# A row maximum compared with the sink as a per-partition scalar, and the attention mask cast once, early, and kept

## The chip, the cores and the metric

The kernel runs on one core of one Trainium2 chip. The metric is the device time of one execution in microseconds (us). Before the change it was 3202.52 us, the median of three runs (3199.64 to 3203.96). Engines are named as in the profile: PE is TensorE, DVE is VectorE, ACT is ScalarE, POOL is GpSimd, SP is SyncE, which issues all the DMAs here.

## What is computed

One step of a two-layer backbone over 1024 latent tokens and 128 context tokens. Layer 0 mixes tokens by differential attention, layer 1 by windowed attention with grouped heads and a sink; a SwiGLU FFN follows each. The change is in layer 1's attention of the latent tokens, where 16 query heads share 4 key/value heads and every block of 128 queries sees 256 cached keys and up to three blocks of its own neighbourhood:

```python
def sink_softmax(s, sink):
    sk = sink.astype(jnp.float32).reshape(SWA_KV_HEADS, SWA_GROUP)[None, :, :, None, None]
    m = jnp.maximum(jnp.max(s, axis=-1, keepdims=True), sk)
    e = jnp.exp(s - m)
    return e / (jnp.sum(e, axis=-1, keepdims=True) + jnp.exp(sk - m))
...
valid = ((k_pos[None, :] >= 0) & (k_pos[None, :] < L)
         & (jnp.abs(q_pos[:, None] - k_pos[None, :]) <= WINDOW))
s_lat = jnp.where(valid, s_lat, NEG_INF)
p = sink_softmax(jnp.concatenate([s_ctx, s_lat], axis=-1), sink).astype(v.dtype)
```

## The kernel before, in words

The program runs in stages: layer 0's modulation and projection (`Start`, `Qkv`), its attention (`diff_attention`), output projection and FFN, then layer 1's projection, its attention (`swa_attention`), output projection and FFN. PE, DVE, ACT and POOL follow the order in which the code is written in most stages (`manual_schedule`); SP is left to the scheduler in all but the first piece.

`swa_attention` cuts the latent work into 32 units: 4 key/value heads times 8 query blocks, with 4 heads in a unit. The string `ROUND` is written out by hand and says which step of which unit is issued next; the last digit of a token is how many units it lies back. For each head of a unit:

- `step_S` (L1015, L1018, L1021) has PE write the scores into one of two PSUM tiles `S`: two matmuls over the cached keys, two over the neighbours, and a bf16 matmul of `mask` by `ident_b` that adds minus 1e30 outside the window. Every `S` ends with that matmul.
- `step_R` (L1026, L1027) has DVE reduce `S` to the negated row maximum `nm`, one number per partition, and then take the smaller of `nm` and the negated sink.
- `step_E` (L1030) has ACT compute the exponential of `S` with `nm` as bias, and the sums. Then `S` is free for the next head.

Then PE transposes the exponentials (L1050), ACT and DVE or POOL split them into a high and a low part (L1059, L1062, L1073; key blocks 0 and 2 go to POOL by L110 and L1073), PE multiplies by V (L1082, L1083), and after a second transposition (L1093, L1098) POOL scales by the reciprocal of the denominator `den` (L1042, L1043, L1102). In every second unit POOL also splits a piece of the output weights (token `W00`, `wo_piece`, L110 and L1114).

At the start of `swa_attention` SP loads the mask (L987), ACT casts it to bf16 (L988) and casts the identity too (L990). `negsink`, the negated sinks of 16 heads on every partition, is made in `small_params`, which is called in the middle of layer 0's projection (slot 20). `junk` is a tile for unwanted elementwise results: `sumsq` (L127) has ACT write squares into it.

Of the kernel before, what the change touches and what calls it, by code (L numbers as in the profile page):

```python
# [9 lines left out]
F32 = mybir.dt.float32  # L10
F32R = mybir.dt.float32r
BF16 = mybir.dt.bfloat16
AF = mybir.ActivationFunctionType
ALU = mybir.AluOpType
# [4 lines left out]
P = 128  # L19
# [25 lines left out]
def hybrid_step(ctx: ExitStack, tc: tile.TileContext, x_prompt, x_sample, cache_diff_k, cache_diff_v,  # L45
# [5 lines left out]
    act, dve, pool, pe = nc.scalar, nc.vector, nc.gpsimd, nc.tensor  # L51
    dma = nc.sync.dma_start
# [15 lines left out]
    const = ctx.enter_context(tc.tile_pool(name="const", bufs=1))  # L68
    ident = const.tile([P, P], F32, name="ident")
# [14 lines left out]
    subg = const.tile([P, 1], F32, name="subg")  # L84
    neglam = const.tile([P, 1], F32, name="neglam")
    negsink = const.tile([P, SH], F32, name="negsink")

    def sbuf(name, side=None):
        return tc.tile_pool(name=name, bufs=1, side=side, reuse_waits="tile")

    def psum(name):
        return tc.tile_pool(name=name, bufs=1, space=PSUM, reuse_waits="tile")
# [348 lines left out]

    def small_params(sb):

        dma(out=subg, in_=diff_subln_g.rearrange("o p -> p o"))
        act.mul(out=subg, in_=subg, mul=1.0 - LAM_INIT)
        lp = sb.tile([P, 4, HD], F32, name="lp")
        dma(out=lp, in_=diff_lambda.rearrange("o f d -> o (f d)").broadcast_to([P, 4 * HD]).rearrange(
            "p (f d) -> p f d", d=HD))
        lpp = sb.tile([P, 2, HD], F32, name="lpp")
        dve.tensor_tensor(out=lpp, in0=lp[:, 0:4:2, :], in1=lp[:, 1:4:2, :], op=ALU.mult)  # L450
        le = sb.tile([P, 2], F32, name="le")
        dve.tensor_reduce(out=le, in_=lpp, axis=AX.X, op=ALU.add)
        act.activation(out=le, in_=le, func=AF.Exp)
        dve.tensor_tensor(out=neglam, in0=le[:, 1:2], in1=le[:, 0:1], op=ALU.subtract)
        dve.tensor_scalar(out=neglam, in0=neglam, scalar1=-LAM_INIT, scalar2=None, op0=ALU.add)
        dma(out=negsink, in_=swa_sink.broadcast_to([P, SH]))
        act.mul(out=negsink, in_=negsink, mul=-1.0)
# [523 lines left out]

    def swa_attention(op, wo_pool, pre, kv0, q0):
        with sbuf("sa") as sb, psum("sap") as ps:

            mask = sb.tile([P, 2, P], BF16, name="mask")
            mraw = sb.tile([P, 2, P], F32, name="mraw")
            dma(out=mraw, in_=swa_mask)  # L987
            act.copy(out=mask, in_=mraw)  # L988
            ident_b = sb.tile([P, P], BF16, name="ident_b")
            act.copy(out=ident_b, in_=ident)  # L990

            class Unit:


# [29 lines left out]
                def step_R(self, h):  # L1024
                    hs, nm = self.g * SG + h, self.nm[:, h:h + 1]
                    dve.tensor_reduce(out=nm, in_=self.S[h][:, self.c0:self.c1], axis=AX.X, op=ALU.max, negate=True)  # L1026
                    dve.tensor_tensor(out=nm, in0=nm, in1=negsink[:, hs:hs + 1], op=ALU.min)  # L1027

                def step_E(self, h):
                    act.activation(out=self.e[:, h, 0:self.nk], in_=self.S[h][:, self.c0:self.c1], func=AF.Exp,  # L1030
# [700 lines left out]
    junk = const.tile([P, D], F32, name="junk")  # L1731
# [126 lines left out]
    with psum("gp0") as ps, sbuf("hT0", "left") as hp, sbuf("wq0", "left") as wq:  # L1858
# [3 lines left out]
        with ExitStack() as early, sbuf("qkv") as sb:  # L1862
# [7 lines left out]
            hooks = {i: ([], [lambda i=i: first.norm(i + 3), lambda i=i: first.load(i + 4)],  # L1870
                         lambda i=i: first.rest(i + 1)) for i in range(NTB)}
            hooks[20] = ([], [lambda: small_params(st)])
            pre0 = []

# [70 lines left out]
    mid.close()  # L1945
    la = Layer(1, pre1)
    la.wo_tiles = swa_attention(la.op, la.wp, *pre1)
    la.begin(ctx)
    before1.close()
# [51 lines left out]
```

## Time and profile before

| | |
|---|---|
| median of three runs | 3202.52 us |
| the profiled execution, its own time | 3199.07 us |
| its span | 3197.3 us |
| PE, DVE, ACT, POOL busy | 3001.8, 2048.6, 1421.9, 1361.9 us |
| granted TensorE clock, mean of the span | 0.981 of full |
| layer 1's latent attention | about 1972 to 2246 us of the span |

The profile is of one execution, so sums are made against 3199.07 us; the median of the runs lies 3.45 us above it. A busy PE is one whose matmuls are in flight, not one at its peak. [...]

### The profile page before, as it was taken

The page shows a single profiled execution, that of the slowest core. Times are in us where ns is not written, and L with a number is a line of the kernel's source. Part 1 is how long each engine was busy: PE and PEld are TensorE (multiplying, and loading weights), DVE is VectorE, ACT ScalarE, POOL GpSimd, SP SyncE. Part 2 cuts the span into 40 slices and gives each one's busy share as a digit, 9 for nine tenths or more (in the row PEclk, how much of TensorE's full clock was granted, in tenths as well). Part 3 has the DMA queues.
Part 4 walks back from the last instruction along what each step waited for, and adds up shares of the span by engine and source line. Part 5 has one row for each costly group of instructions (what it writes and reads, how often), then busy time and mean ns, then how long its engine had stood idle before and what let it go on. Part 6 is the DMA issues. An engine that isn't in the chain of part 4 may idle for free.

```text
span 3197.3 us, 47914 instructions
## 1 busy us (share of the span) xinstructions
PE 3001.8 (94%) x17998; PEld 2636.8 (82%) x17998; DVE 2048.6 (64%) x2789; ACT 1421.9 (44%) x2764; POOL 1361.9 (43%) x1186
## 2 busy tenths in 40 slices
PE   8999988998896999999999899999987999999999
PEld 5888777777776999999878787777767999998887
DVE  6786388888566777753786643999567633334544
ACT  6332267777554333333444323777433333333442
POOL 2553289999343444442021343666333433340101
PEclk9999999999998999999999999999988999999999
DMA  6675633332422434335765354433432322226564
GB/s 214 200 228 179 201 112 114 116 118 94 130 100 80 129 109 129 109 97 177 252 216 195 130 173 125 116 115 99 142 107 81 108 64 83 66 80 211 185 199 149
DMA packets 373808, 442.23 MB, mean 138 GB/s; under 512 B 26804, under 2 KB 295644, under 8 KB 373576
## 3 DMA queue, kind: packets, MB, share of 16 engines
q1 hardware_dynamic: 373576, 439.16, 43.6%
q8 instruction: 142, 2.33, 0.3%
q14 instruction: 90, 0.74, 0.1%
HBM read 335.71 MB, written 103.37 MB: 137 GB/s over the span
## 4 chain that ended last, share of the span: by engine, by line
PE 67%; POOL 14%; DVE 9%; ACT 4%; issue 3%; DMA 2%; SPq 1%; DVEq 0%; ACTq 0%; POOLq 0%
POOL aT L784 7%; PE guX L1518 6%; PE guX L1519 6%; PE guX L1520 6%; PE dacc L1635 5%; PE dacc L1637 5%; PE dacc L1636 5%; POOL aT L110 4%; PE qacc L556 4%; PE qacc L558 4%; PE qacc L557 4%; PE guY L1518 3%; PE guY L1520 3%; PE guY L1519 3%; PE guZ L1518 1%
## 5 line engine op out<-in xcount | busy, mean ns | idle before, releaser
L1551 POOL TENSOR_TENSOR sg<-sg,U 128x256 f32<-128x256 f32 x88 | 74.9, 851 | 563.4 <-ACT sg L1550 553.1
L1635 PE MATMUL dacc<-fh,ahl 128*128 128x512 f32 x792 | 312.0, 394 | 2.3 <-DVE U L1554 2.3
L1636 PE MATMUL dacc<-fl,ahl 128*128 128x512 f32 x792 | 310.7, 392 | 0.0
L1637 PE MATMUL dacc<-fh,ahl 128*128 128x512 f32 x792 | 310.7, 392 | 0.0
L556 PE MATMUL qacc<-whi,hh 128*128 128x512 f32 x648 | 259.7, 401 | 1.3 <-ACT hh L431 1.3
L558 PE MATMUL qacc<-whi,hl 128*128 128x512 f32 x648 | 254.9, 393 | 0.0
L557 PE MATMUL qacc<-wlo,hh 128*128 128x512 f32 x648 | 254.2, 392 | 0.6 <-DVE wlo L106 0.6
L154 POOL TENSOR_TENSOR xt<-yacc,xt 128x1024 f32<-128x1024 f32 (+1 forms) x19 | 49.7, 2621 | 459.9 <-DVE yacc L153 242.0
L784 POOL TENSOR_TENSOR aT<-a,aT 128x512 fp32r<-128x512 f32 x186 | 237.3, 1276 | 15.5
L1620 DVE TENSOR_TENSOR fl<-fraw,fh 128x1024 fp32r<-128x1024 f32 x132 | 165.4, 1253 | 121.3 <-ACT fh L1619 120.7
L744 DVE TENSOR_REDUCE nm<-S 128x1 f32<-128x1280 f32 x128 | 190.2, 1486 | 51.1 <-PE S L737 51.1
L1619 ACT CAST fh<-fraw 128x1024 fp32r<-128x1024 f32 x132 | 138.4, 1048 | 170.8 <-DMA fraw<-in_w_down_dram 156.7
L737 PE MATMUL S<-K,q 128*128 128x512 f32 (+1 forms) x768 | 184.5, 377 | 12.9 <-ACT e L749 8.9
L266 DVE SCALAR_TENSOR_TENSOR macc<-wmod,sc,macc 128x512 f32<-128x512 f32 x196 | 186.1, 992 | 0.0
L1635 PEld LDWEIGHTS dacc<-fh,ahl 128*128 128x128 f32 x792 | 149.2, 188 | 36.4 <-DVE U L1554 3.1
L1637 PEld LDWEIGHTS dacc<-fh,ahl 128*128 128x128 f32 x792 | 149.0, 188 | 33.7
L1636 PEld LDWEIGHTS dacc<-fl,ahl 128*128 128x128 f32 x792 | 149.1, 188 | 32.9
L749 ACT ACTIVATE e<-S,nm 128x1280 f32<-128x1280 f32 x128 | 171.4, 1339 | 7.2 <-DVE nm L744 7.1
L737 PEld LDWEIGHTS S<-K,q 128*128 128x128 f32 x768 | 137.5, 193 | 43.8 <-ACT e L749 19.0
L578 ACT CAST xT<-tpx 128x512 fp32r<-128x512 f32 x127 | 68.5, 592 | 236.5 <-issue 125.3
L110 POOL TENSOR_SCALAR aT<-a 128x512 fp32r<-128x512 f32 x192 | 154.0, 802 | 22.7 <-ACT a L773 22.7
L1490 DVE TENSOR_TENSOR fl<-fsum,fh 128x1024 fp32r<-128x1024 f32 x84 | 102.3, 1218 | 81.3 <-ACT fh L1488 81.3
(369 smaller groups left out, 9726.7 us busy)
## 6 DMA issues: line engine op xcount, KB each, us to landing
fraw<-in_w_down_dram SPq DMA_DIRECT2D x132, 512.0 KB
wmod<-in_w_mod_dram SPq DMA_DIRECT2D x112, 256.0 KB
araw<-a_d SPq DMA_DIRECT2D x132, 192.0 KB
fraw<-in_w_gate_dram SPq DMA_DIRECT2D x44, 512.0 KB
fraw<-in_w_up_dram SPq DMA_DIRECT2D x42, 512.0 KB
qT_d<-xT SPq DMA_DIRECT2D x36, 512.0 KB
q<-qT_d SPq DMA_DIRECT2D x64, 256.0 KB
wraw<-in_w_qkv_diff_dram SPq DMA_DIRECT2D x24, 512.0 KB
```

The lines of the kernel that those rows point to most:

```text
L110: pool.tensor_scalar(out=out, in0=in_, scalar1=1.0, scalar2=0.0, op0=ALU.mult, op1=ALU.add)
L556: pe.matmul(acc, lhsT=xh, rhs=hi[:, a, :], start=(kb == 0), stop=False)
L557: pe.matmul(acc, lhsT=xh, rhs=lo[:, a, :], start=False, stop=False)
L558: pe.matmul(acc, lhsT=xl, rhs=hi[:, a, :], start=False, stop=(kb == KB - 1))
L737: pe.matmul(S[:, j:j + n], lhsT=self.q[:, f, m, i * P:(i + 1) * P], rhs=kv[self.h][0][:, m, j:j + n], start=(f == 0), stop=(f == 1))
L784: (dve if self.last else pool).tensor_tensor(out=lo, in0=x, in1=hi.bitcast(F32), op=ALU.subtract)
L1518: pe.matmul(o, lhsT=hi[:, kb, :], rhs=xh[:, kb, :], start=(first and kb == 0), stop=False, **more)
L1519: pe.matmul(o, lhsT=hi[:, kb, :], rhs=xl[:, kb, :], start=False, stop=False, **more)
L1520: pe.matmul(o, lhsT=lo[:, kb, :], rhs=xh[:, kb, :], start=False, stop=(kb == 3), **more)
L1635: pe.matmul(acc, lhsT=ah, rhs=hi[:, cs], start=(d == 0), stop=False)
L1636: pe.matmul(acc, lhsT=ah, rhs=lo[:, cs], start=False, stop=False)
L1637: pe.matmul(acc, lhsT=al, rhs=hi[:, cs], start=False, stop=(d == NDF - 1))
```

## The change

The mask and the bf16 identity become tiles that live as long as the program. They are made in `small_params`, with `junk` as the landing place of the raw mask. The comparison of the maximum with the sink becomes a tensor_scalar: `negsink`'s column is the scalar operand, one value per partition, where it was a second tensor of one element per partition.

```diff
@@ hybrid_step, constants
+    mask = const.tile([P, 2, P], BF16, name="mask")
+    ident_b = const.tile([P, P], BF16, name="ident_b")
@@ small_params
+        mraw = junk[:, 0:2 * P].rearrange("p (a k) -> p a k", k=P)
+        dma(out=mraw, in_=swa_mask)
+        act.copy(out=mask, in_=mraw)
+        act.copy(out=ident_b, in_=ident)
         dma(out=subg, in_=diff_subln_g.rearrange("o p -> p o"))
@@ swa_attention
-            mask = sb.tile([P, 2, P], BF16, name="mask")
-            mraw = sb.tile([P, 2, P], F32, name="mraw")
-            dma(out=mraw, in_=swa_mask)
-            act.copy(out=mask, in_=mraw)
-            ident_b = sb.tile([P, P], BF16, name="ident_b")
-            act.copy(out=ident_b, in_=ident)
@@ step_R
-                    dve.tensor_tensor(out=nm, in0=nm, in1=negsink[:, hs:hs + 1], op=ALU.min)
+                    dve.tensor_scalar(out=nm, in0=nm, scalar1=negsink[:, hs:hs + 1], scalar2=None, op0=ALU.min)
```

On DVE each of 128 rows `TENSOR_TENSOR nm<-nm,negsink 128x1` becomes `TENSOR_SCALAR nm<-nm,negsink 128x1` in the same place; PE and POOL keep their order. On ACT two casts move. At the start of layer 1's attention, ACT before (xT is a transposed piece of q, k or v):

```order
L578 CAST xT<-tpx 128x512 x4
L601 COPY qout<-qacc 128x512
L578 CAST xT<-tpx 128x512 x4
L990 CAST ident_b<-ident 128x128
L988 CAST mask<-mraw 128x256
L1030 ACTIVATE e,den<-S,nm 128x512 x4
```

and now:

```order
L585 CAST xT<-tpx 128x512 x4
L608 COPY qout<-qacc 128x512
L585 CAST xT<-tpx 128x512 x4
L1029 ACTIVATE e,den<-S,nm 128x512 x4
L1039 ACTIVATE es<-es 128x4
```

The two casts are gone from between the last xT and the first exponential. They stand now in layer 0's projection on ACT, ahead of `subg`:

```order
L105 CAST mhi<-macc 128x512 x2
L585 CAST xT<-tpx 128x512 x2
L449 CAST mask<-junk 128x256
L450 CAST ident_b<-ident 128x128
L452 ACTIVATE subg<-subg 128x1
L460 ACT_TABLE_LOAD
L460 ACTIVATE le<-le 128x2
```

where before the second of these rows was followed by `subg` at once. On SP the load of the mask stood before in layer 1, between the last pieces of q on their way out and the loads for the next units:

```order
L970 DMA V<-v_d_63 128x11x128
L518 DMA wraw<-in_w_qkv_swa_dram 128x2x512
L579 DMA qT_d_59<-xT 128x8x128 x13
L987 DMA mraw<-in_swa_mask_dram 128x256
L977 DMA q<-qT_d_59 128x4x256
L978 DMA q<-qT_d_59 64x4x256
```

and stands now in layer 0's projection, between a load of weights and a store of q:

```order
L586 DMA qT_d_58<-xT 128x8x128
L525 DMA wraw<-in_w_qkv_diff_dram 128x2x512
L448 DMA junk<-in_swa_mask_dram 128x256
L586 DMA qT_d_58<-xT 128x8x128
L525 DMA wraw<-in_w_qkv_diff_dram 128x2x512
```

It has moved past the whole of layer 0, and the loads of q that stood behind it in layer 1 are each one place nearer.

## Rows read from the trace of the kernel before

**Rows 1.** Page, part 1: busy time and share of each engine.
```profile
PE 3001.8 (94%) x17998; PEld 2636.8 (82%) x17998; DVE 2048.6 (64%) x2789; ACT 1421.9 (44%) x2764; POOL 1361.9 (43%) x1186
```
**Rows 2.** Windows: length, busy us of PE, PEld, DVE, ACT, POOL, PEclk, DMA share, GB/s.
```profile
1970.00:1974.00 4.00, 1.39 (x12) 1.31 (x13) 1.12 (x2) 2.27 (x6) 0.00 (x0) 1.00 0.48 133
1974.00:1988.00 14.00, 9.22 (x37) 7.42 (x37) 5.78 (x16) 5.39 (x14) 1.05 (x2) 0.51 0.86 262
2000.00:2236.00 236.00, 219.87 (x1511) 183.12 (x1510) 216.49 (x425) 179.23 (x425) 153.42 (x174) 1.00 0.38 112
```
**Rows 3.** Timeline at that attention's start: start, duration, work [idle before <- releaser].
```profile
1972.89 0.31 ACT L990 CAST ident_b<-ident 128x128 bf16<-128x128 f32 x1
...
1973.48 0.54 SPq L987 DMA_DIRECT2D mraw<-in_swa_mask_dram  x1
...
1976.83 0.40 ACT L988 CAST mask<-mraw 128x256 bf16<-128x256 f32 x1 [3.63 <-DMA mraw<-in_swa_mask_dram]
1977.29 0.26 PE L1021 MATMUL S<-mask,ident_b 128*128 128x128 bf16 x1 [4.55 <-ACT mask L988]
```
**Rows 4.** Waits from 2000 to 2236 us: who for whom, us in total, times, longest.
```profile
ACT e L1030 <- DVE nm L1027: 50.6, 42, 2.6
...
PE S L1015 <- ACT e L1030: 15.7, 12, 1.5
```
**Rows 5.** Line L1027: duration in ns, least, median, greatest.
```profile
L1027 DVE TENSOR_TENSOR nm<-nm,negsink x128: 158/229/1118, 1978.3 to 2236.1; 128x1 f32<-128x1 f32 x128
```
**Rows 6.** Timeline of one of the twelve stalls, and L1027 in the last.
```profile
2065.93 1.29 POOL L1114 TENSOR_TENSOR wol<-wraw,woh 128x512 fp32r<-128x512 f32 x1
...
2066.39 0.84 DVE L1042 TENSOR_TENSOR den<-den,es 128x4 f32<-128x4 f32 x1
...
2067.88 1.27 POOL L1073 TENSOR_TENSOR pT<-a,pT 128x512 fp32r<-128x512 f32 x1
...
2068.19 0.98 DVE L1027 TENSOR_TENSOR nm<-nm,negsink 128x1 f32<-128x1 f32 x1
...
2069.26 0.79 ACT L1030 ACTIVATE e<-S,nm 128x640 f32<-128x640 f32 x1 [2.49 <-DVE nm L1027]
...
2070.20 0.50 PE L1015 MATMUL S<-K,q 128*128 128x256 f32 x2 [1.43 <-ACT e L1030]
...
2232.44 1.11 DVE L1027 TENSOR_TENSOR nm<-nm,negsink 128x1 f32<-128x1 f32 x1
```
**Rows 7.** Other DVE lines: duration in ns, least, median, greatest.
```profile
L1043 DVE RECIPROCAL den<-den x32: 177/178/180, 1985.4 to 2239.4; 128x4 f32<-128x4 f32 x32
L153 DVE SCALAR_TENSOR_TENSOR xn<-oacc,rs,q x18: 740/746/752, 850.7 to 972.6; 128x512 f32<-128x512 f32 x18
L264 DVE TENSOR_SCALAR macc<-wmod,sc x28: 470/1402/1519, 1023.3 to 2491.6; 128x512 f32<-128x512 f32 x28
L918 DVE COPY s_all<-s x2: 170/390/611, 862.5 to 874.3; 128x4 f32<-128x4 f32 x2
L455 DVE TENSOR_SCALAR neglam<-neglam x1: 154/154/154, 188.8 to 188.8; 128x1 f32<-128x1 f32 x1
L756 DVE SCALAR_TENSOR_TENSOR s<-s_all,neglam,s x64: 218/359/572, 398.5 to 797.7; 128x1 f32<-128x1 f32 x64
```
**Rows 8.** Windows at the first layer's attention start, columns as in rows 2.
```profile
389.00:394.00 5.00, 0.55 (x4) 0.30 (x2) 1.93 (x3) 1.67 (x2) 0.00 (x0) 0.97 0.87 255
394.00:404.00 10.00, 8.90 (x23) 6.99 (x24) 7.29 (x7) 4.54 (x9) 0.00 (x0) 0.50 1.00 330
404.00:414.00 10.00, 6.60 (x39) 5.13 (x37) 9.47 (x10) 7.36 (x12) 7.38 (x7) 1.00 0.26 76
```
**Rows 9.** Timeline of the first projection, where the load and the casts now stand.
```profile
85.88 1.07 ACT L127 ACTIVATE junk<-xin 128x1024 f32<-128x1024 f32 x1
...
89.50 0.37 SPq L579 DMA_DIRECT2D qT_d<-xT  x1
...
187.96 0.20 ACT L453 ACTIVATE le<-le 128x2 f32<-128x2 f32 x1 [4.81 <-DVE le L452]
```

## The prediction

> **What bounds the kernel now.** I read the page's busy times first. PE is busy for 3001.8 us of the span, 94%, and no other engine for more than 64% [rows 1]: the kernel is bound by PE nearly everywhere, and a change of small DVE and ACT work is worth only what PE idles because of it. So I went to the stage that the change touches, the latent attention of layer 1, and asked two things: when does PE idle there, and what ended each idle time.
>
> The windows cut the stage in two [rows 2]. From 2000 to 2236 us, 236 us of steady work, PE is busy for 219.87 us, so it idles for 16.1 us. [...]
>
> The timeline of the start shows the first thing [rows 3]. The scores of the first head are there but for the mask's matmul, and PE then idles for 4.55 us until the cast of the mask ends. The cast waited 3.63 us for the mask's load, and that load left SP only at 1973.48. Nothing else of this head is late: its q and K were there, since their matmuls had run.
>
> The waits show the second [rows 4]. In the steady part, PE's idle time is one wait: 12 times, 15.7 us, longest 1.5, for an exponential of ACT, whose end gives a score tile back. ACT in turn waited 42 times, 50.6 us, for `nm` of L1027, the comparison with the sink. That instruction handles one element per partition, and yet takes from 158 to 1118 ns [rows 5].
>
> The timeline of one stall shows why [rows 6]. POOL's L1114, the split of a piece of output weights, runs from 2065.93 to 2067.22. DVE's L1042, four elements, starts at 2066.39 and ends at 2067.23, as L1114 ends. The reduction follows, POOL's L1073 runs from 2067.88 to 2069.15, and L1027, started at 2068.19, ends at 2069.17, again with POOL. ACT starts its exponential only then, after idling for 2.49 us, and PE gets its tile after idling for 1.43 us. So a DVE instruction with two tensors in SBUF stands still while POOL works. All 12 stalls lie in units with a weight piece, and in each of them L1027 takes 0.98 to 1.12 us; the last is at 2232.44.
>
> **The change, part by part.**
>
> *The load and the casts at the start go.* PE's idle time of 4.55 us covers both casts and the load [rows 3], so it goes whole: the mask's matmul can follow its predecessors at once. Late next is the loop of two score tiles, which is paced by reduction, comparison and exponential with or without the change, so the whole start moves forward by 4.55 us. The bound below is 3.5 us, if 1 us of it is lost again to a q that now lands too late; the bound above is 4.55.
>
> *The clock at the start.* In the first layer's attention PE was busy for 0.55 us in five, the clock fell, and it stayed at 0.50 through ten us in which PE was busy for 8.90; in the ten after that PE was busy for 6.60 at 1.00 [rows 8]. [...] Before the change the second attention's start shows PE busy for 1.39 us in four ahead of the fall [rows 2]. Without the 4.55 us hole the next scores come straight after, and the start is more like the 6.60 in ten: I expect no fall. The 9.22 busy us after 1974 were all at about half speed, so at full speed they are 4.6 us shorter at most. At first PE alternates with DVE and ACT, whose steps do not shrink, so I take 2.0 us; the ends are 0 (the clock falls anyway) and 4.6.
>
> *The load and the casts in their new place.* SP's load stands between a load of weights and the store at 89.50 [rows 9]. It must wait until ACT's last squares in `junk` end (85.88 + 1.07 = 86.95), and takes 0.54 us of SP [rows 3]: it is out by about 87.5, 2 us before the store behind it is ready to go. Of the engines only ACT's cast waits for it, and that one stands almost 100 us further down. The casts are 0.40 and 0.31 us [rows 3]; ACT idles for 4.81 us ahead of L453, which stands just behind [rows 9], and this idle time takes them up. I cost both at nothing. If that cover were gone, at most 0.7 us would reach PE.
>
> *The comparison.* Free of POOL, what does the new form cost? With a constant scalar one such instruction took 154 ns; the nearest instruction with a scalar per partition, L756, took 218 at least [rows 7]; the old form takes 158 at least [rows 5]. The scalar per partition seems to add some 60 ns, so I take 0.21 us, between 0.154 and 0.218. Where POOL is idle this makes the change a loss of 0.05 us for each comparison. In the start some four of them are in the loop, 0.2 us in all; in the steady part they lie beside PE's work.
>
> Does the new form wait for POOL? This decides. For no: a reciprocal, one tensor in SBUF, takes 177 to 180 ns in all 32 cases of this very stage; and L153, which has a scalar per partition, one tensor in SBUF and one in PSUM, takes 740 to 752 in all 18 [rows 7]. So neither a single tensor nor a scalar per partition brings the wait. For yes: a tensor_scalar over 512 elements from SBUF to SBUF takes 470 ns at least but 1402 at the median, and a copy of four elements took 170 once and 611 once [rows 7], so some instructions with a single tensor do wait. The trace has a single tensor_scalar of one element, 154 ns [rows 7], too few to tell. The reciprocal's row is nearest in size and operands, so I take no wait. [...]
>
> Without the wait, a stall shrinks by what L1027 stood still. The twelve sum to 12.3 us (from 0.98 to 1.12 each, as in rows 6), and 12 x 0.21 = 2.5 remain, so 9.8 us go, of PE's 15.7 [rows 4]. The rest stays: L1042 keeps two tensors and its wait of 0.84 us for L1114, and this is what is late next [rows 6]. The ends are 0 (the new form waits too) and 15.7 (nothing is left).
>
> **Sum.** -4.55 - 2.0 + 0.2 - 9.8 = -16.2 us against the profiled execution's 3199.07. The median of the runs stands 3.45 us higher; carried over to it, 3202.5 - 16.2 = 3186.3, and I say 3186.5. Within the forecast its ends are -9 (3.5 from the start, no clock, 6 from the stalls) and -22.
>
> **The rivals.**
>
> *The new form waits for POOL as the old one did.* Then the stalls stay, each longer by 0.05 us, 0.6 us in all, and only the start gains: -4.55 - 2.0 + 0.2 + 0.6 = -5.75, or 3196.8; 3198.8 if the clock falls as before. For it speak the median of L264 and the copy of four elements; against it the reciprocals. It lies within 0.2% of the time before (6.4 us, about what a measurement of this kernel can tell from no change).
>
> *The new form waits longer than the old one.* POOL's two steps on a piece follow each other closely; a form that needs POOL to be out of the way altogether could miss the gap between them, and stand still for a second POOL instruction, 1.27 us in rows 6. In 12 stalls that is 15.2 us, less the 6.35 of the start: +8.9, or 3211.4. It decides from about half a us more per stall. Against it: L264's longest, 1519 ns, is 1.05 above its shortest [rows 7], which is less than one POOL instruction.
>
> *The mask's wait is only replaced* by one for the next units' q and K. Their loads stood behind the mask's on SP, so they leave half a us sooner, but are wanted 4.55 us sooner. Then the start's 6.35 go and 9.8 stay: 3192.7. This lies inside the forecast's own range, and speaks only for its upper part.
>
> **How the numbers follow.** The forecast, with the last case in it, has 0.70; the new form waiting as the old one 0.24; waiting longer 0.06. The likeliest alone spans 3180 to 3193. The range has to reach the first rival's 3196.8 and 3198.8 to leave out no more than 2 in 10, so it is 3180 to 3199. Every part of the forecast lies beyond 0.2%, so faster has 0.70; the first rival is no change, 0.24; slower 0.06.
>
> **What would show it.** In the profile after, 128 comparisons near 0.21 us with hardly any spread; PE's wait for L1030's exponential in the steady part down from 15.7 to about 6 us, and ACT's wait for `nm` to less than half; no wait of PE for a mask; the granted clock at 1.00 through the start; in layer 0's projection, ACT's casts ahead of `subg` and no new wait of PE. The forecast is wrong if the comparisons still reach 1 us (first rival) or 1.5 us and more (second), or if PE's idle time in the steady part stays near 16 us although they are short, which would mean that something else than L1027 holds ACT.

## The result, and the profile after

The changed kernel takes 3183.52 us at the median of four runs (3178.57 to 3185.64), beside 3202.15 for the kernel before on the same chip: a ratio of 0.994, 95% interval 0.9923 to 0.9957. It is faster by 18.6 us. The forecast was 3186.5.

From here on, "the stage" runs from the first S matmul of layer 1's latent attention to the last pair of them over the neighbours, "the start" from the first S matmul to the first AV matmul, and "the steady part" from there to the stage's end. These three instants can be read to a hundredth of a microsecond in any of the traces, so they cut all kernels alike. The lines of the kernel after stand one lower than before: L1027 is now L1026, L1030 is L1029, L1042 is L1041.

The windows of the kernel before, cut this way (columns as in [rows 2]):

```profile
1972.03:1990.85 18.82, 12.65 (x64) 10.18 (x63) 8.03 (x20) 9.32 (x23) 2.09 (x3) 0.64 0.76 223
1990.85:2234.82 243.97, 227.51 (x1558) 188.94 (x1558) 223.96 (x440) 185.45 (x439) 158.86 (x179) 1.00 0.39 112
```

And those of the kernel after:

```profile
1975.79:1989.35 13.56, 10.43 (x63) 8.32 (x63) 8.23 (x20) 8.57 (x21) 2.08 (x3) 0.87 1.01 301
1989.35:2221.09 231.74, 224.60 (x1558) 188.97 (x1558) 205.21 (x440) 186.58 (x439) 158.25 (x179) 1.00 0.41 118
```

The start falls from 18.82 to 13.56 us, the steady part from 243.97 to 231.74: 5.26 and 12.23, together 17.5 us. That is nearly the whole fall of the median. (The two profiled executions differ by only 13.4 us in span; the one after reached the stage 3.76 us later. The third run below, and the other profiles, show no delay that stands out of the scatter.)

The comparison itself, line L1026, answers to [rows 5]: least, median and greatest in ns.

```profile
L1026 DVE TENSOR_SCALAR nm<-nm,negsink x128: 212/214/217, 1977.3 to 2222.3; 128x1 f32<-128x1 f32 x128
```

The 128 comparisons now differ by 5 ns, where they differed by 960 ns. DVE's busy time on the page falls by 18.6 us against [rows 1], and PE's is unchanged at 94%:

```profile
PE 3003.8 (94%) x17998; PEld 2640.7 (83%) x17998; DVE 2030.0 (64%) x2789; ACT 1423.5 (45%) x2764; POOL 1363.3 (43%) x1186
```

The waits of the steady part after, which answer to [rows 4]:

```profile
ACT e L1029 <- DVE nm L1026: 37.9, 37, 1.7
...
PEld S L1014 <- ACT e L1029: 12.0, 13, 1.2
PE S L1014 <- ACT e L1029: 6.3, 12, 0.8
```

PE still stalls 12 times, but for 6.3 us in place of 15.7 (over the whole steady part as cut here, the kernel before has 13 waits and 15.9 us). One of these stalls on the timeline (start, duration, work, idle before it) answers to [rows 6]:

```profile
2060.74 1.29 POOL L1113 TENSOR_TENSOR wol<-wraw,woh 128x512 fp32r<-128x512 f32 x1
...
2060.95 1.10 DVE L1041 TENSOR_TENSOR den<-den,es 128x4 f32<-128x4 f32 x1
...
2062.18 0.79 DVE L1025 TENSOR_REDUCE nm<-S 128x1 f32<-128x640 f32 x1
...
2062.70 1.28 POOL L1072 TENSOR_TENSOR pT<-a,pT 128x512 fp32r<-128x512 f32 x1
2063.01 0.21 DVE L1026 TENSOR_SCALAR nm<-nm,negsink 128x1 f32<-128x1 f32 x1
2063.32 0.79 ACT L1029 ACTIVATE e<-S,nm 128x640 f32<-128x640 f32 x1 [1.71 <-DVE nm L1026]
...
2064.25 0.51 PE L1014 MATMUL S<-K,q 128*128 128x256 f32 x2 [0.74 <-ACT e L1029]
```

The comparison runs through in 0.21 us in the middle of POOL's L1072 (L1073 before), with which L1027 used to end. What is late now is L1041 ahead of it: it starts at 2060.95 and ends at 2062.05, as POOL's piece of weights ends at 2062.03. The reduction and the comparison queue behind it on DVE.

At the start, no wait of PE for the mask is left. The mask's load is issued 87.51 us into the span and takes SP 0.34 us, and PE has no new wait in the first projection.

### The profile page after: what moved, and what is told of

Its sections match the earlier page's. It is cut to its first block, busy times and chain, and to the rows that moved or that the text cites. A ratio compares the mean times of both kernels' runs of the same rounds, so it can differ in the third digit from the quotient of the medians.

```text
span 3183.9 us, 47914 instructions
## 1 busy us (share of the span) xinstructions
PE 3003.8 (94%) x17998; PEld 2640.7 (83%) x17998; DVE 2030.0 (64%) x2789; ACT 1423.5 (45%) x2764; POOL 1363.3 (43%) x1186
## 4 chain that ended last, share of the span: by engine, by line
PE 58%; DVE 7%; ACT 3%; issue 2%; POOL 2%; DMA 1%; DVEq 0%; ACTq 0%; POOLq 0%
PE guX L1517 6%; PE guX L1518 6%; PE guX L1519 6%; PE dacc L1634 5%; PE dacc L1635 5%; PE dacc L1636 5%; PE guY L1517 3%; PE guY L1519 3%; PE guY L1518 3%; PE guZ L1517 1%; PE guZ L1519 1%; PE guZ L1518 1%; PE tpp L1049 1%; PE qacc L563 1%; PE qacc L565 1%
```

## The experiments

Three questions were open. Do the two parts act by themselves, and is each worth what the forecast gave it? Why does the new form not wait for POOL? And does the fall of PE's waits account for the whole fall of the steady part? Each run was timed against the kernel before on its chip: 3202.96 us at the median for the three runs with one part at a time and for the one with the addition on POOL, 3203.07 for the one with two equal elements and for the two without low weights, 3201.41 for the one with two neighbouring elements.

### One part at a time

The new comparison alone:

```
 kernel before
-  dve.tensor_tensor(out=nm, in0=nm, in1=negsink[:, hs:hs + 1], op=ALU.min)
+  dve.tensor_scalar(out=nm, in0=nm, scalar1=negsink[:, hs:hs + 1], scalar2=None, op0=ALU.min)
```

> The kernel before with the new form of the comparison alone; the mask is loaded and cast where it was, in the second layer's attention. Theory (the two parts are independent): all 128 comparisons take 0.21 to 0.22 us, PE's wait for ACT's exponential in the steady part falls from 15.7 us to about 6.3 as in the changed kernel, and the start stays as before, with PE's 4.55 us wait for the mask and the clock down over 1974 to 1988. The time falls by the 12.2 us of the steady part, less at most 0.2: about 3190 (3188 to 3193). Rival (the mask's move shifts the phases of the rounds, and part of the steady gain is its doing): the comparisons are as short, but the fall is 6 us or less, 3196 or more.

Measured: 3188.33 us, ratio 0.9953 (0.9941 to 0.9965), so 14.6 below before. Its windows, start and steady part:

```profile
1972.31:1991.29 18.98, 12.61 (x63) 10.09 (x63) 8.41 (x20) 9.34 (x23) 2.08 (x3) 0.64 0.75 221
1991.29:2223.23 231.94, 224.70 (x1559) 189.01 (x1558) 205.62 (x440) 186.64 (x439) 158.47 (x179) 1.00 0.41 118
```

The steady part is that of the changed kernel to within 0.2 us, the start that of the kernel before to within 0.2 us, the clock at the start included (0.64 of full in both). The rival, that the mask's move was part of the steady gain, is refuted.

The mask's move alone:

```
 kernel after
-  dve.tensor_scalar(out=nm, in0=nm, scalar1=negsink[:, hs:hs + 1], scalar2=None, op0=ALU.min)
+  dve.tensor_tensor(out=nm, in0=nm, in1=negsink[:, hs:hs + 1], op=ALU.min)
```

> The changed kernel with the old form of the comparison, so the mask's move alone. Theory: PE never waits for the mask, first S to first AV falls from 18.8 us to about 13.6, the comparisons spread from 158 to over 1000 ns again and PE's wait for the exponential is back at 15 to 16 us. The time falls by 5.3: about 3197 (3195 to 3199). If the two parts are independent, the falls of this run and of the one with the new comparison alone add up to that of the changed kernel, 17.5 us in the stage. Rival (the clock at the start falls whatever the mask does, and earlier work only runs into it): a fall of 1 to 3 us, 3199 to 3201.

Measured: 3197.93 us, ratio 0.9985 (0.9976 to 0.9993), 5.0 below before. The windows:

```profile
1973.35:1985.94 12.59, 8.96 (x63) 7.09 (x63) 8.54 (x21) 8.60 (x21) 2.14 (x3) 1.00 1.00 301
1985.94:2229.86 243.92, 227.29 (x1558) 188.84 (x1558) 223.89 (x438) 185.66 (x439) 159.03 (x179) 1.00 0.39 113
```

The start falls by 6.23 us, and the steady part is that of before within 0.05. The stage of this run is shorter by 6.3 us than before's and that of the first by 11.9: together 18.2, beside the changed kernel's 17.5 in its first profile and 18.7 in the next run's. The parts add up.

The changed kernel once more:

> The changed kernel once more, for the comparison with the others on one chip and for the 3.8 us by which its first profile reached the second layer's attention later than that of before. Theory (scatter of single executions, nothing of the change): the time of arrival at the first S matmul lies within 1.5 us of before's 1972.0, while first S to last S is 245 us as in the first profile; fall of the median 17 us (15 to 20). Rival (the mask's load and cast in the first projection, or the buffer that now stays allocated, delays the first layer): the arrival is 3 us late again, at 1975 or later, and the fall stays at 17 or less against a stage that gains 17.5.

Measured: 3184.26 us, ratio 0.9942 (0.9929 to 0.9954), 18.7 below before. The windows:

```profile
1974.04:1986.35 12.31, 8.92 (x64) 7.09 (x63) 8.34 (x20) 8.60 (x21) 2.15 (x3) 1.00 1.01 293
1986.35:2218.09 231.74, 224.54 (x1559) 188.97 (x1559) 205.32 (x440) 186.52 (x439) 158.36 (x179) 1.00 0.41 120
```

This execution reached the stage at 1974.04, 2.0 us after before's, between my two expectations. The other profiles decide it: with the mask moved they arrive from 1969.68 to 1977.38, with it in its old place from 1972.03 to 1974.78. The early load and cast show no delay that stands out of this scatter. The start is shorter here than in the first profile, by the clock alone, which is taken up below.

### What makes the comparison wait

Over two elements, one read twice:

```
 kernel after
+  self.nm2 = sb.tile([P, SG, 2], F32, name="nm2", tag="nm2", bufs=4)
...
-  dve.tensor_scalar(out=nm, in0=nm, scalar1=negsink[:, hs:hs + 1], scalar2=None, op0=ALU.min)
+  dve.tensor_scalar(out=self.nm2[:, h, :], in0=nm.broadcast_to([P, 2]), scalar1=negsink[:, hs:hs + 1],
+                    scalar2=None, op0=ALU.min)
...
```

> The changed kernel with the same comparison by the scalar of each partition, over two equal elements instead of one (the minimum read twice, its result written twice; the exponential and the sinks take the first). [...] Rival (what waits is the form with two arrays in SBUF, and the scalar form never does): 0.21 to 0.23 us throughout, and a time within 2 us of the changed kernel's.

Measured: 3204.24 us, ratio 1.0006 (0.9997 to 1.0015): nothing of the gain is left. The comparison, the steady window and the steady waits:

```profile
L1027 DVE TENSOR_SCALAR nm<-nm,negsink x128: 228/253/1347, 1978.9 to 2244.8; 128x2 f32<-128x2 f32 x128
```

```profile
1991.16:2243.52 252.36, 229.68 (x1559) 188.43 (x1558) 232.85 (x440) 184.48 (x439) 159.23 (x179) 1.00 0.38 108
```

```profile
PEld S L1015 <- ACT e L1031: 34.6, 33, 1.9
...
PE S L1015 <- ACT e L1031: 22.2, 21, 1.5
```

The same operation with the same scalar per partition, one element longer, stands still up to 1347 ns. It costs more than the old form, 252.36 us of steady part against 243.97, and eats what the mask's move gives; I had expected the old form's price at most (3197, and 16 us of PE's wait where 22.2 came). POOL is what it waits for: 20 of these comparisons take 0.99 us or more, where the old form had 12 over 0.9, and each of the 20 ends within 0.03 us of POOL's L1074, the split of the probabilities. Why it meets that split more often than the old form is not shown. The count of elements it is, then, unless the repeated read did it. So two different neighbours, in place (the edit shown against the run just told):

```
+  pairs = [sb.tile([P, SG, 2], F32, name=f"nm2{i}") for i in range(4)]
+  for t in pairs:
+      pool.memset(t, 0.0)
...
-  dve.tensor_scalar(out=self.nm2[:, h, :], in0=nm.broadcast_to([P, 2]), scalar1=negsink[:, hs:hs + 1],
+  dve.tensor_scalar(out=self.nm2[:, h, :], in0=self.nm2[:, h, :], scalar1=negsink[:, hs:hs + 1],
```

> The comparison by the scalar of each partition over two different neighbouring elements, read and written in place (the maximum and a zero beside it, from tiles that POOL clears once at the start), in place of one element read twice. Theory (the count of free elements decides): the comparisons stand still as with the element read twice, mean 0.36 to 0.47 us, some over 1.1, and PE waits 14 to 23 us in the steady part, which takes 242 to 254 us; time 3196 to 3206. Rival (it was the repeated read, a stride of zero, that made that run slow): 0.21 to 0.23 us throughout, the steady part at 231.7 and the time within 2 us of the changed kernel's.

Measured: 3204.78 us, ratio 1.0013 (1.0003 to 1.0023). The comparison, and the steady part:

```profile
L1030 DVE TENSOR_SCALAR nm<-nm,negsink x128: 228/254/1329, 1973.0 to 2240.5; 128x2 f32<-128x2 f32 x128
```

```profile
1985.39:2239.28 253.89, 231.18 (x1558) 189.59 (x1558) 232.40 (x440) 184.71 (x439) 159.13 (x179) 0.99 0.37 107
```

PE's wait there is 22.3 us in 21, and 20 comparisons take 0.99 us or more, each ending within 0.03 us of POOL's split of the probabilities. (The steady part is also a little longer for the clock, which stood at 0.89 of full from 1995 to 2010 us.) That is much the same as with the repeated read, so the repeated read was not it. The same operation with the same scalar per partition took 212 to 217 ns over one element and up to 1347 and 1329 ns over two. Why the second element makes it wait is not shown, and no run here has three or more.

### Whose work the waits were for

The kernel before, and then the one after, without POOL's subtraction for each piece of output weights. The low part of these weights is left out of the last projection; the high part stands in its place.

```
 kernel before, and kernel after
-  wo = [[wo_pool.tile([P, D], F32R, name=f"wo{f}{kb}") for f in "hl"] for kb in range(KB)]
+  wo = [[wo_pool.tile([P, D], F32R, name=f"woh{kb}")] * 2 for kb in range(KB)]
...
-  hi, lo = wo[kb][0][:, cs], wo[kb][1][:, cs]
-  pool_round(hi, raw)
-  pool.tensor_tensor(out=lo, in0=raw, in1=hi.bitcast(F32), op=ALU.subtract)
+  pool_round(wo[kb][0][:, cs], raw)
```

> The kernel before without the low part of the second layer's output weights: POOL's subtraction for each piece is left out (the high part stands for both), so the last projection is computed from less exact weights. Theory (the old comparisons stood still beside POOL's subtraction of 1.1 to 1.3 us in each piece): without it the 12 long comparisons fall to the length of the rounding or less, PE's wait for the exponential falls from 15.7 to 4 or less, and the time falls by 10 to 14, 3188 to 3192. Rival (any work of POOL in that place, the rounding of the piece or the split of the probabilities, does it): the longest comparisons stay near 1.1 us and the fall is under 6.

Measured on the kernel before: 3181.05 us, ratio 0.9937 (0.9922 to 0.9952), 22.0 below before. Its comparisons, its steady part and the waits there:

```profile
L1027 DVE TENSOR_TENSOR nm<-nm,negsink x128: 158/256/828, 1981.1 to 2222.1; 128x1 f32<-128x1 f32 x128
```

```profile
1993.59:2220.85 227.26, 226.43 (x1559) 189.35 (x1558) 209.22 (x440) 184.85 (x439) 139.11 (x164) 1.00 0.42 120
```

```profile
PEld S L1015 <- ACT e L1030: 7.8, 25, 0.7
...
PE S L1015 <- ACT e L1030: 0.3, 1, 0.3
```

The comparisons beyond 0.83 us are gone, and with them PE's 12 stalls. But the expectation named the wrong work of POOL. In the kernel before, each of the 12 long comparisons ends within 0.03 us of L1073, POOL's split of the probabilities, as in [rows 6]; it is the addition ahead of them, L1042, whose 12 long cases (0.83 and 0.84 us) end with the subtraction L1114. By the order of these rows, the subtraction matters by holding that addition and by standing ahead of L1073 in POOL's queue. Without it the addition takes 155 ns at most, and the longest comparisons, 0.82 and 0.83 us, still end with L1073. So the rival, that POOL's other work holds the comparisons too, is right as to what holds them and wrong as to the price.

The time fell by more than I expected (its interval puts the fall between 15 and 25 us), and the steady part by 16.7, though PE's wait had only 15.9 to give. That surplus led to the loader's rows, below.

> The changed kernel without the low part of the second layer's output weights, left out in the same way. Theory (what is left of PE's stalls comes from the addition of the denominators, which stands still beside the same subtraction): the longest addition falls from 1187 ns to 850 or less, PE's wait from 6.3 us to 2 or less, the time to 3178 to 3181. Rival (the stalls left are of another cause): 5 to 6 us of wait remain, the time within 2 us of 3183.5.

Measured on the kernel after: 3170.75 us, ratio 0.9908 (0.9891 to 0.9924), 32.3 below before and below the 3178 to 3181 that I expected. The addition of the denominators, the steady part and the loader's wait:

```profile
L1041 DVE TENSOR_TENSOR den<-den,es x32: 151/152/157, 1977.1 to 2208.7; 128x4 f32<-128x4 f32 x32
```

```profile
1982.00:2204.38 222.38, 221.56 (x1559) 189.58 (x1559) 195.06 (x440) 187.21 (x439) 138.97 (x164) 1.00 0.44 125
```

```profile
PEld S L1014 <- ACT e L1029: 1.4, 5, 0.5
```

Without the subtraction the addition is never over 157 ns, where 12 of the changed kernel's take from 0.88 to 1.19 us, each ending within 0.03 us of the subtraction (L1113), and PE idles for 0.82 us in all. What is left of the stalls after the change is that addition beside that subtraction. The fall of the steady part is 9.4 us, again more than PE's 6.3.

### Where the fall beyond PE's idle time comes from

PE's row counts a wait only where no matmul is in flight. The loader's row (PEld) shows the same wait from the moment the weights of the next S could have been loaded. For the kernel before, in the same steady part:

```profile
PEld S L1015 <- ACT e L1030: 24.9, 26, 1.9
PE S L1015 <- ACT e L1030: 15.9, 13, 1.5
```

Twenty-six waits, of which PE's row shows 13. Two of the others, on the timeline of POOL, DVE and the loader, from a unit without a weight piece:

```profile
2059.22 0.62 POOL L110 TENSOR_SCALAR pT<-a 128x512 fp32r<-128x512 f32 x1 [1.58 <-ACT a L1059]
...
2059.35 0.48 DVE L1027 TENSOR_TENSOR nm<-nm,negsink 128x1 f32<-128x1 f32 x1
...
2060.87 0.30 PEld L1015 LDWEIGHTS S<-K,q 128*128 128x128 f32 x2 [0.33 <-ACT e L1030]
...
2061.16 0.61 POOL L1102 TENSOR_TENSOR ol<-ol,den 128x256 f32<-128x256 f32 x1
...
2061.20 0.58 DVE L1027 TENSOR_TENSOR nm<-nm,negsink 128x1 f32<-128x1 f32 x1
...
2062.75 0.30 PEld L1015 LDWEIGHTS S<-K,q 128*128 128x128 f32 x2 [0.27 <-ACT e L1030]
```

The first comparison ends at 2059.83, with POOL's rounding of probabilities (2059.84), the second at 2061.78, with POOL's scaling of an output (2061.77). Comparisons of about half a microsecond, held by such shorter meetings with POOL (its split of the probabilities most often), make the loader 0.2 to 0.5 us late; PE has a matmul in flight then and counts as busy, but the next one starts late all the same. PE's own busy time shows it too: for the same matmuls at the same clock, 1.00, it falls from 227.51 to 224.60 us from before to after. The two rows against the length of the steady part:

| kernel | steady part | loader's wait for ACT's exponential | PE's |
|---|---|---|---|
| before | 243.97 | 24.9 in 26 | 15.9 in 13 |
| mask's move alone | 243.92 | 25.2 in 26 | 16.2 in 13 |
| over two elements | 252.36 | 34.6 in 33 | 22.2 in 21 |
| after | 231.74 | 12.0 in 13 | 6.3 in 12 |
| before, no low weights | 227.26 | 7.8 in 25 | 0.3 in 1 |
| after, no low weights | 222.38 | 1.4 in 5 | none |

From before to after, the loader's wait falls by 12.9 us and PE's by 9.6; the steady part falls by 12.2. The steady part less the loader's wait is 218 to 221 us in all six rows; less PE's wait it is 222 to 230. The loader's row is the better account, though not an exact one: against before, its sum and the steady part change by the same to within 2 us in these rows.

### A version that beats both

The addition goes to POOL, and the reciprocal to the step that reduces the transposed output:

```
 kernel after
-  dve.tensor_tensor(out=self.den, in0=self.den, in1=self.es, op=ALU.add)
-  dve.reciprocal(out=self.den, in_=self.den)
+  pool.tensor_tensor(out=self.den, in0=self.den, in1=self.es, op=ALU.add)
...
 def step_D(self, _):
+  dve.reciprocal(out=self.den, in_=self.den)
```

> The changed kernel with the sum of the denominators put on POOL, behind the pieces that it waited for on DVE, and the reciprocal put behind the transposed output's reduction on DVE. Theory (the addition, up to 1187 ns long on DVE beside POOL's pieces of the output weights, is what now holds up the comparisons and so the exponential): PE's 12 stalls before S in the steady part go from 6.3 us to about 1, and the time falls by 4 to 6 below the changed kernel, 3178 to 3180 against its 3183.5. Rival (the exponential is as late for ACT's own order, or the reduction before the comparison is): the stalls stay at 5 to 6 us and the time is within 2 us of the changed kernel's. A second rival: the reciprocal or the multiplication behind it now comes late for POOL, whose queue then stands, and the time rises above 3184.

Measured: 3173.21 us, ratio 0.9908 (0.9895 to 0.9922), 29.8 below before and 11.0 below the changed kernel on the same chip. Its windows, its waits and the addition on POOL:

```profile
1972.65:1984.96 12.31, 8.92 (x63) 7.09 (x63) 8.20 (x18) 8.60 (x21) 2.34 (x4) 1.00 1.01 303
1984.96:2207.09 222.13, 221.36 (x1558) 189.89 (x1558) 190.18 (x409) 187.94 (x439) 162.62 (x208) 1.00 0.42 124
```

```profile
ACT e L1029 <- DVE den L1095: 25.5, 29, 1.1
...
PE av L1080 <- ACT oT L1085: 0.6, 2, 0.4
PEld S L1014 <- ACT e L1029: 0.5, 1, 0.5
...
ACT e L1029 <- DVE nm L1026: 0.4, 1, 0.4
```

```profile
L1041 POOL TENSOR_TENSOR den<-den,es 128x4 f32<-128x4 f32 x32 | 6.4, 201 | 15.1 <-ACT es L1039 15.1
```

On POOL the addition takes 201 ns and never meets POOL's other work, since it stands in the same queue. PE idles for 0.77 us of the 222.13: the steady part is now bound by PE's own work. The gain is about twice what I expected, for I had again counted PE's row (6.3 us) and not the loader's (12.0, now 0.5). POOL's own wait for ACT's `es` is harmless: neither rival shows.

## Why the prediction was right, and where it was off

**The new form does not wait** [rows 5, 7]. Right, and it decided the case: 212 to 217 ns against 0.21 taken. The choice rested on the reciprocals, which are of four elements and took 177 to 180 ns in all 32 cases. The two runs over two elements show that the likeness went only so far: a tensor_scalar of one tensor waits here over two elements (up to 1347 and 1329 ns), as L264's median, 1402 ns against 470 at least, had hinted. So the step from the reciprocals was in part luck: the same likeness would have spoken for a pair as well, and there it would have been wrong. What decided in these runs, one element or two, did not enter the sum. The first rival would have been right for a pair, and even the second in part: a pair makes the loader wait more often (33 against 26 times) and takes 8.4 us more than the old form, but its longest comparison, 1347 ns, shows no stand for a second POOL instruction.

**The twelve stalls, -9.8** [rows 4, 6]. PE's wait fell from 15.7 to 6.3 us, by 9.4, and what is left is L1042's addition, as said, which now stands still for up to 1.19 us where it was 0.84. The mis-sized step is the one that stopped there: "a stall shrinks by what L1027 stood still", summed over the twelve that PE's row shows. The shorter waits of L1027, 0.4 to 0.6 us, each ending with a step of POOL on the probabilities or the output, were left out of the sum. The loader was late for them too, and the steady part gave 12.2 us.

**ACT's wait for `nm` to less than half.** Wrong: 50.6 us (52.2 over the whole steady part) became 37.9. Most of what is left is slack of ACT that costs PE nothing: in the version with the addition on POOL, ACT still waits 25.5 us for DVE (put down there to the reciprocal that follows the comparison), and PE never waits for the exponential in the steady part.

**The mask's wait, -4.55** [rows 3]. Right. PE's wait for the mask is gone in every run with the move, and the loads of q and K are not late next: what PE waits for in the new start is the exponential, the loop of two score tiles that the prediction named. PE's waits for it over the start, in the kernel before, in the changed kernel's first profile and in its second:

```profile
PE S L1015 <- ACT e L1030: 1.5, 2, 0.7
...
PE S L1014 <- ACT e L1029: 3.0, 3, 1.3
...
PE S L1014 <- ACT e L1029: 3.4, 3, 1.3
```

**The clock at the start, -2.0** [rows 2, 8]. The range of 0 to 4.6 held; "I expect no fall" was half right. Without the move the clock fell in all three profiled executions (0.64, 0.64, 0.73 of full over the start). With it, it stayed at full (1.00) in four (the mask's move alone, the changed kernel's second profile, the addition on POOL, and the one after without the low weights) and fell for some three microseconds in three (0.87 and 0.88 over the start). Without a fall the start takes 12.31 us in the changed kernel, 6.5 less than before, where the prediction said 6.35; with it 13.56, 5.26 less. The split comes out too, by the rows: without a fall PE is busy for 3.7 us less in the start (8.92 against 12.65), but waits 1.9 us more for the exponential, so the clock gives about 1.8 net beside the mask's 4.55. No run moves the mask with the clock held, so this split is worked out and not measured by itself. In the starts of before and after, ACT's exponentials over 512 keys take 0.69 us and DVE's reductions of as many 0.68 to 0.69 at either clock, while the first pair of S matmuls of a head takes 0.47 to 0.51 us at full and 0.78 to 0.80 at half: as the prediction had it, only PE's steps shrink. The 0.2 us for longer comparisons is too small to tell: the new form's start is longer by 0.16 us without the move (18.98 against 18.82) and shorter by 0.28 with it (12.31 against 12.59).

**The sum.** The forecast was -16.2 us against the profiled execution; the stage gave 17.5 and 18.7 in two executions. The steady part gave 2.4 us more than the sum had, by the short waits; the start gave 1.1 less with a fall of the clock and 0.2 more without. The median came out 3.0 us below the forecast. The far end of the forecast, -22, is not worked out in the prediction: the far ends of its parts add up to -24.7.

**The new place of the load and casts, 0.** Nothing in the runs speaks against it: the load leaves SP at 87.51 us, as worked out, and ACT's idle time behind the casts is still 4.33 us, where it was 4.81.

## What to carry to other kernels

A tiny instruction on DVE that takes anything from its least to several times that while POOL works (here 158 to 1118 ns) is worth rewriting where PE waits on it, and the form decided: here one tensor, one scalar per partition and one element ran in 212 to 217 ns every time, and with one element more (up to 1347 ns) the gain was gone. Where PE waits for a chain, sum the loader's waits as well as PE's, since PE's row leaves out waits that a matmul in flight covers (here it had 13 of 26); the time followed the larger sum. And when an instruction meets another engine's long work, putting it into that engine's own queue can be cheaper: here 201 ns, where waiting from outside took up to 1187 ns.

## What the runs showed of the hardware

The clock at the start went either way in the same program: 0.87 of full over the start in one execution, 1.00 in the other. The two profiles of the changed kernel have the same waits up to the point where they part. The first, with the clock at half (0.50 of full) from about 1981.2 to 1984.6:

```profile
1978.46 0.51 PE L1014 MATMUL S<-K,q 128*128 128x256 f32 x2 [1.31 <-ACT e L1029]
...
1981.18 0.80 PE L1014 MATMUL S<-K,q 128*128 128x256 f32 x2 [1.05 <-ACT e L1029]
```

And the second, with none:

```profile
1976.71 0.51 PE L1014 MATMUL S<-K,q 128*128 128x256 f32 x2 [1.31 <-ACT e L1029]
...
1979.43 0.50 PE L1014 MATMUL S<-K,q 128*128 128x256 f32 x2 [1.06 <-ACT e L1029]
```

PE waited 1.31 us and then 1.05 or 1.06, with the same matmuls between; the first pair of S matmuls after that took 0.80 us in the one and 0.50 in the other. What tips it stays open.

The steady part repeated far better here than the work ahead of the stage: it took 243.97 and 243.92 us with the old comparison, and 231.74, 231.94 and 231.74 with the new, while the same five executions reached the stage anywhere between 1972.0 and 1975.8. Here the stage resolved what a single span could not.
